# Products with the values for eight heads in one visit, five load buffers and nine probability tiles

## The chip, the cores and the metric

The kernel runs on one core of a Trainium2 chip. The metric is the device time of one execution in microseconds (us), as the median of several runs. A core has five engines that run side by side, each with its own instruction stream: TensorE (PE; its weight loads are shown apart as PEld), VectorE (DVE), ScalarE (ACT), GpSimd (POOL) and SyncE (SP). They wait for one another by semaphores. Transfers between the large memory and the on-chip memory are issued by an engine and carried out by DMA engines. TensorE writes to PSUM, which the kernel uses as eight banks of 2 KB per partition; all else lies in the on-chip memory of 128 partitions.

## What is computed

The reference is a trunk of two layers over 256 tokens of 1024 numbers. Each layer takes a normalised input, projects it to all that three branches need, runs the branches, merges them by gates and adds the result. Cut to what matters here:

```python
for layer in range(2):
    h = rms_norm(x, norm_w[layer])
    proj = einsum('bsd,de->bse', h, w_in[layer])
    (a_xbc, a_z, a_dt, b_q, b_k, b_v, b_z,
     c_q, c_k, c_v, c_f, c_z, gates) = split(proj)
    y_a = mamba2_branch(...)                 # a chunked scan
    y_b = sliding_window_branch(...)         # 16 heads, window 128, sinks
    y_c = forgetting_attention_branch(...)   # 16 heads, causal, decay bias
    branch = einsum('bsiw,iwd->bsid', stack(y_a, y_b, y_c), w_proj[layer])
    x = x + einsum('bsd,de->bse', sum(g * branch), w_out[layer])
return rms_norm(x, final_norm_w)

# in both attention branches
probs = softmax(scores)
out = einsum(probs, v)
return out * silu(z)
```

Heads are 64 wide, so each attention branch has 16 heads of 256 queries. With blocks of 128 tokens a head has three blocks of probabilities: the first query block against the first key block, and the second against both.

## The kernel before

**Dense projections.** Nearly all of TensorE's time goes to the projections. Activations and weights are each split into a rounded high part and a rest, and each product is made of three: high by high, low by high, high by low (`dense`, L275, and `dense2`). A 1024-row weight matrix is taken in column pieces, and each piece in parts of 512 KB or less, 274 parts in all. A part goes through three steps: SyncE issues its load into a `raw` buffer (`load_part`, L321 to L332, the issue on L330); ScalarE rounds it into a `hi` buffer (L261); VectorE subtracts to make the `lo` buffer (L262). After that the raw buffer is free.

`feed` keeps four split parts ahead of TensorE (`AHEAD`), and after each split it asks `load_to` for the load of the part that is `N_RAW` further on. All loads are on SyncE's queue in the order of the parts, so load j waits for the lo of part j - `N_RAW`, and everything after it on that queue waits too. In the start (L1226, L1230) parts are split in halves.

**Side work.** Attention, the scan and the norms are written as generators. They are advanced between dense pieces, from `pump`, by a planner with a clock of its own in estimated microseconds: a generator yields either a delay, or the name of a token, or a condition, and is advanced when it is due and what it waits for holds. The order of TensorE's instructions that comes out of this is kept by the program. VectorE, ScalarE and GpSimd follow the written order only in the start; afterwards a scheduler sets theirs. In what follows, a stretch of side work on TensorE between two dense matmuls is called a visit.

**PSUM.** Dense results rotate over three banks (`pmm`), side work over five (`pmx`).

**Attention.** `attn_quad` (L534) handles four heads and is used 16 times: four times per layer by `swa_quad` (L611) for the sliding window and four times by `fox_quad` (L862) for the other. In order it

- takes the token `pp` (one for two buffers of scores), makes the scores in four PSUM banks with 64-row tiles in one visit;
- does the softmax: VectorE adds the bias and takes the extreme (L561), ScalarE the exponential (L567), VectorE scales (L579);
- transposes twelve 128x128 blocks in two visits of six, and ScalarE copies them to three tiles of 2 KB per partition (L596). These are tag `L2`, which the scan, the gates and others also use;
- gives `pp` back, then waits for `gated`, which says that the gate values for these heads are there;
- makes the products with the values in one bank `py`: 8 matmul instructions, each with 64 columns of weights, so that two heads go to the lower and upper half of the partitions;
- multiplies by the gate on VectorE (L609).

In the traces a product visit is recorded as 16 matmuls "mx<-L,L" with the tile shape 128*64 and 256 columns as the first record's shape.

**The scan.** `ssd_group` (L706) does four heads, eight groups in all over the two layers. It may begin when no sliding-window attention of its layer is waiting, and holds one token `ssd`. Its last visit has 24 records, also of 128*64, and takes a new bank four times. Where the text speaks of the third branch's attention, it is `fox_quad`'s.

**The end of a layer.** `out_end` adds the residual (L1003), squares (L217) and, after the last piece, normalises the rows for the next layer; its transposes and splits then feed the next layer's first dense matmuls.

Buffers are counted by tag in `BUFS` (L59).

Of the kernel before, what the change touches and what calls it, by code (L numbers as in the profile page):

```python
# [14 lines left out]
ALU = mybir.AluOpType  # L15

P = 128
S = 256
# [8 lines left out]
D_GN1, D_GN2, D_CUM, D_H, D_M = 4.0, 6.0, 12.0, (4.8, 6.4), 5.0  # L27
BUDGET = 1.35
T_PP, T_SSD, T_BIAS = 1, 1, 1
N_RAW, N_SPLIT = 6, 6  # L30
AHEAD = 4
WARM = 10
FILL = 10
# [11 lines left out]
def hybrid_trunk(  # L45
# [10 lines left out]
    ps = ctx.enter_context(tc.tile_pool(name="ps", bufs=1, space=bass.MemoryType.PSUM))  # L56
    dr = ctx.enter_context(tc.tile_pool(name="dr", bufs=1, space=bass.MemoryType.DRAM))

    BUFS = dict(raw=N_RAW, hi=N_SPLIT, lo=N_SPLIT, L8=8, L4=2, L2=7, L1=14, pp=2, qt=4,  # L59
                bias=2, st=2, sm=6)  # L60
    count = [0]

    def T(tag, shape, dtype=F32, bufs=None):
        count[0] += 1
        return sb.tile(shape, dtype, tag=tag, name=f"{tag}_{count[0]}",
                       bufs=bufs if bufs is not None else BUFS.get(tag, 1))

    def PS(tag, bufs):
        count[0] += 1
        return ps.tile([P, 512], F32, tag=tag, name=f"{tag}_{count[0]}", bufs=bufs)  # L70
# [4 lines left out]
    def pmx():  # L75
        return PS("mx", 5)
# [3 lines left out]
    tt = nc.vector.tensor_tensor  # L80
# [10 lines left out]
    def mm(o, a, b, **kw):  # L91
        n = b.free_size()
        if a.dtype == F32R:
            clock["t"] += max(0.094, n / 2350.0)
        else:
            clock["t"] += max(0.2, n / 587.0) * (0.5 if a.free_size() == 64 else 1.0)
        nc.tensor.matmul(o, a, b, **kw)  # L97

    def transpose(o, a, i):
        clock["t"] += 0.109  # L100
        nc.tensor.transpose(o, a, i)  # L101
# [91 lines left out]
    def bc(ap, axis, n):  # L193
        s = list(ap.shape)
        s.insert(axis, n)
        return ap.unsqueeze(axis).to_broadcast(s)
# [192 lines left out]
    for l in range(L):  # L389
        y = Layer()  # L390
# [140 lines left out]
            yield 0.0  # L531
        return f

    def attn_quad(qTs, kTs, biases, nsink, v, vcols, sz, gated, scored=lambda: None):  # L534


        yield "pp"
        pps = [T("pp", [P, 2, 3 * P]) for _ in range(2)]
        nm = T("nm", [P, 8], bufs=2)
        sums = T("sums", [P, 8], bufs=2)  # L540
        blocks = ((0, slice(0, P)), (1, slice(P, 3 * P)))

        scs = [pmx() for _ in range(4)]

        def score(p, i, b):
            return scs[2 * p + i][:, b * P:P + 2 * P * b]

        for p in range(2):
            for b in range(2):
                for i in range(2):  # L550
                    r = slice(64 * i, 64 * i + 64)
                    mm(score(p, i, b), qTs[p][r, b * P:(b + 1) * P], kTs[p][r, 0:(b + 1) * P],
                       start=True, stop=True)
        for p in range(2):
            pp = pps[p]
            ps_ = slice(4 * p, 4 * p + 4)
            ns = None if nsink is None else nsink[:, 2 * p:2 * p + 2]
            for i in range(2):
                for b, sl in blocks:
                    e = 4 * p + 2 * i + b  # L560
                    nc.vector.tensor_tensor_reduce(  # L561
                        out=pp[:, i, sl], in0=score(p, i, b), in1=biases(p, i, b), scale=-0.125,
                        scalar=1.0e30 if ns is None else ns[:, i:i + 1],
                        op0=ALU.add, op1=ALU.min, accum_out=nm[:, e:e + 1])
                for b, sl in blocks:
                    e = 4 * p + 2 * i + b
                    act(pp[:, i, sl], pp[:, i, sl], AF.Exp, scale=-1.0, bias=nm[:, e:e + 1],  # L567
                        accum_out=sums[:, e:e + 1])
            if nsink is not None:
                es = T("es", [P, 4], bufs=2)  # L570
                tt(es.rearrange("p (i b) -> p i b", i=2), nm[:, ps_].rearrange("p (i b) -> p i b", i=2),
                   bc(ns, 2, 2), op=ALU.subtract)
                act(es, es, AF.Exp)
                tt(sums[:, ps_], sums[:, ps_], es, op=ALU.add)
            rs = T("rsum", [P, 4], bufs=4)
            nc.vector.reciprocal(rs, sums[:, ps_])
            for i in range(2):
                for b, sl in blocks:
                    ts(pp[:, i, sl], pp[:, i, sl], rs[:, 2 * i + b:2 * i + b + 1], 0.5,  # L579
                       op0=ALU.mult, op1=ALU.mult)  # L580
        yield D_SOFT
        scored()

        order = [(0, 0), (0, 1), (1, 0), (1, 1), (0, 2), (1, 2),
                 (2, 0), (2, 1), (2, 2), (3, 0), (3, 1), (3, 2)]
        at = {hb: (n // 4, n % 4 * P) for n, hb in enumerate(order)}
        pTs = []
        for n, (h, b) in enumerate(order):
            if n == 6:
                yield D_SOFT2  # L590
            if n % 4 == 0:
                pt = pmx()
            transpose(pt[:, n % 4 * P:(n % 4 + 1) * P], pps[h // 2][:, h % 2, b * P:(b + 1) * P], ident)
            if n % 4 == 3:
                pT = T("L2", [P, 512])
                act(pT, pt, AF.Copy)  # L596
                pTs.append(pT)
        yield D_EVAC
        tokens["pp"] += 1
        yield gated  # L600
        sz = sz()
        py = pmx()
        for p in range(2):
            for b, o in ((0, 0), (1, P)):
                for i in range(2):
                    n, c = at[2 * p + i, 2 * b]
                    mm(py[64 * i:64 * i + 64, S * p + o:S * p + S], v[:, b, vcols(p, i)],
                       pTs[n][:, c:c + S - o], start=(b == 0), stop=(b == 1))
        tt(sz, py.rearrange("p (u s) -> p u s", u=2), sz, op=ALU.mult)  # L609

    def swa_quad(y, c, qT):  # L611
        yield lambda: (1, 0) in y.zdone or (y.l == 0 and y.rn is None)
        yield from attn_quad(
            [qT[:, j, :] for j in range(2)], [y.kT[:, c, :]] * 2,
            lambda p, i, b: wmask[:, P:2 * P] if b == 0 else wmask,
            y.nsink[:, 4 * c:4 * c + 4], y.bv, lambda p, i: slice(64 * c, 64 * c + 64),
            lambda: y.sz[1][:, 2 * c:2 * c + 2, :], lambda: (1, 2 * c + 1) in y.zdone)
# [244 lines left out]
    def fox_quad(y, j):  # L862
        yield "bias"
        bs = []
        for p in range(2):
            bias = T("bias", [P, 2, 3 * P])
            nc.scalar.dma_start(bias[:, :, P:3 * P],
                                y.cumd[2 * (j + p):2 * (j + p) + 2, 1, :].partition_broadcast(P))
            bs.append(bias)
        yield D_BDMA  # L870
        for bias in bs:
            for dst, src in ((slice(0, P), slice(P, 2 * P)), (slice(2 * P, 3 * P), slice(2 * P, 3 * P))):
                for i in range(2):
                    nc.gpsimd.affine_select(out=bias[:, i, dst], in_=bias[:, i, src],  # L874
                                            compare_op=ALU.is_ge, fill=NEG, base=0,
                                            pattern=[[-1, P]], channel_multiplier=1)
        yield lambda: j + 1 in y.cqdone and clock["t"] >= y.cqdone[j + 1] + D_BIAS
        kqs = [y.ckT[j], y.ckT[j + 1]]

        def scored():  # L880
            tokens["bias"] += 1

        yield from attn_quad([kq[:, 1, :] for kq in kqs], [kq[:, 0, :] for kq in kqs],
                             lambda p, i, b: bs[p][:, i, P * b:P + 2 * P * b], None, y.cv,
                             lambda p, i: slice(P * (j + p) + 64 * i, P * (j + p) + 64 * i + 64),
                             lambda: y.sz[2][:, j:j + 2, :], lambda: (2, j + 1) in y.zdone, scored)
# [169 lines left out]
    def sub(src, n=256):  # L1056
        subs.append((src, n))
        return len(subs) - 1
# [5 lines left out]
    for y in layers:  # L1064
# [2 lines left out]
        y.rn = None  # L1067
        y.gate, y.qT, y.ckT, y.sz, y.yh, y.yl, y.sq, y.h, y.ss, y.var, y.zdone, y.cqdone = {}, {}, {}, {}, {}, {}, [], {}, {}, {}, set(), {}
        y.u = y.cv = None

        def cols(c0, n=256):
            return sub([(0, w[:, c0:c0 + n])], n)
# [30 lines left out]
        if l == 0:  # L1103
            k, v = cols(C_BK), cols(C_BV)
# [47 lines left out]
        o = [sub([(0, w_out[l, :, c:c + n])], n) for c, n in ((0, 256), (256, 512), (768, 256))]  # L1152
# [36 lines left out]
    with tc.manual_schedule(engines={ENG.PE, ENG.DVE, ENG.Activation, ENG.Pool}):  # L1189
# [10 lines left out]
        p = pmx()  # L1200
# [90 lines left out]
        for k in (0, 2):  # L1291
# [4 lines left out]
        v = T("sm", [P, 8])  # L1296
        nc.vector.tensor_reduce(v[:, 0:2], ss.rearrange("p (t j) -> p t j", t=2), axis=mybir.AxisListType.X,
                                op=ALU.add)
# [51 lines left out]
```

## Time and profile before

| what | value |
|---|---|
| median of 3 runs | 840.01 us (839.77 to 840.1) |
| the profiled execution's own time | 839.45 us |
| span in that profile | 837.7 us |
| mean granted TensorE clock | 0.999 |
| split of raw parts to hi, L261 | 262 times, 264.1 us busy on ScalarE |
| rest to lo, L262 | 262 times, 312.7 us busy on VectorE |
| loads of 512 KB for the input projection | 179, median 4.6 us from issue to landing |
| moved by DMA | 157.99 MB, mean 189 GB/s |

The span is what the profile's rows cover; the execution's own time is 1.75 us longer. Rows of a timeline give the start in us from the span's start, the duration, the engine, line and operation, then out<-in with the names of the program, the shape of the tile and the columns, and the number of records put together in the row. In square brackets stands the idle time before it and what ended it. Rows of a window give the length of the stretch, then the busy time and the instructions (x) of the engines named, then granted clock, the DMA share and GB/s. Matmuls are pipelined and their ends are modelled, so durations of two matmuls overlap, and the differences between starts are what counts. Rows of waits give total us, number of times and longest.

### The profile page before, as it was taken

How to read it: one execution, taken by the hardware profiler on the slowest of the kernel's cores; microseconds unless marked ns; L12 is line 12 of the kernel's file. 1: busy time of each engine (PE TensorE's matmuls, PEld its weight loads, DVE VectorE, ACT ScalarE, POOL GpSimd, SP SyncE). 2: the span in 40 equal slices, each digit the busy share in tenths (PEclk: the TensorE clock that was granted, in tenths of full speed). 3: DMA queues.
4: the chain of work that ended last, by engine and by line, in shares of the span. 5: the costliest groups of instructions: out<-in, count | busy, mean ns of one | idle time of the engine just before them, and what ended most of it. 6: DMA issues, size and time to landing. Idle time of an engine off the chain costs nothing.

```text
span 837.7 us, 16280 instructions
## 1 busy us (share of the span) xinstructions
PE 828.7 (99%) x6067; PEld 767.2 (92%) x6067; DVE 650.2 (78%) x1426; ACT 510.9 (61%) x1022; POOL 102.3 (12%) x141
## 2 busy tenths in 40 slices
PE   8999999999999999999999999999999999999996
PEld 8999999989999998888999999999899999988896
DVE  6987898998766679665787688899968667785665
ACT  7477768665666657443654676876557567654442
POOL 1810000000221010220024000100003110121000
PEclk9999999999999999999999999999999999999999
DMA  9775467676565556665676544765756564476632
GB/s 307 220 216 169 119 185 229 204 214 203 153 198 176 153 165 203 207 221 186 211 247 213 152 121 147 226 216 187 247 175 183 155 189 151 153 238 214 214 101 76
DMA packets 123113, 157.99 MB, mean 189 GB/s; under 512 B 5746, under 2 KB 90090, under 8 KB 123034
## 3 DMA queue, kind: packets, MB, share of 16 engines
q1 hardware_dynamic: 108816, 140.53, 53.6%
q10 hardware_dynamic: 13962, 16.37, 6.2%
q8 instruction: 48, 0.79, 0.4%
q14 instruction: 31, 0.25, 0.1%
q0 software_dynamic: 256, 0.05, 0.0%
HBM read 154.76 MB, written 2.16 MB: 187 GB/s over the span
## 4 chain that ended last, share of the span: by engine, by line
PE 98%; DMA 1%; DVE 0%; SPq 0%; POOLq 0%; issue 0%; ACT 0%
PE mm L97 84%; PE mx L97 9%; PE mx L101 4%; DMA L<-in_x_dram 1%; SPq L330 0%; SPq L164 0%; DVE L L1214 0%; POOLq L1346 0%; ACT L L1028 0%; DVE L L1222 0%; DVE L L1003 0%; DVE L L1007 0%; DVE sm L230 0%; DVE rs L232 0%; DVE sm L256 0%
## 5 line engine op out<-in xcount | busy, mean ns | idle before, releaser
L262 DVE TENSOR_TENSOR lo<-raw,hi 128x1024 fp32r<-128x1024 f32 (+3 forms) x262 | 312.7, 1208 | 85.8 <-ACT hi L261 75.4
L97 PE MATMUL mm<-hi,L 128*128 128x512 f32 (+4 forms) x1424 | 376.5, 352 | 0.2
L97 PE MATMUL mm<-L,hi 128*128 128x256 f32 x1792 | 318.0, 279 | 0.0
L261 ACT ACTIVATE hi<-raw 128x1024 fp32r<-128x1024 f32 (+3 forms) x262 | 264.1, 1022 | 84.7 <-PE mm L97 76.6
L97 PEld LDWEIGHTS mm<-L,hi 128*128 128x128 f32 x1792 | 277.9, 192 | 7.4 <-issue 3.9
L97 PEld LDWEIGHTS mm<-hi,L 128*128 128x128 f32 x1424 | 251.0, 190 | 26.3 <-issue 2.1
L97 PE MATMUL mm<-lo,L 128*128 128x512 f32 (+4 forms) x712 | 247.1, 348 | 0.0
L97 PE MATMUL mm<-L,lo 128*128 128x256 f32 x896 | 246.7, 275 | 0.0
L97 PEld LDWEIGHTS mm<-L,lo 128*128 128x128 f32 x896 | 172.1, 192 | 0.2
L97 PEld LDWEIGHTS mm<-lo,L 128*128 128x128 f32 x712 | 134.6, 190 | 12.3
L874 POOL TENSOR_SCALAR_AFFINE_SELECT bias<-bias 128x128 f32<-128x128 f32 x64 | 34.1, 569 | 409.5 <-DMA bias<-cumd 291.1
L567 ACT ACTIVATE pp<-pp,nm 128x128 f32<-128x128 f32 (+1 forms) x128 | 56.6, 444 | 13.2 <-DVE nm L561 11.2
L696 DVE SCALAR_TENSOR_TENSOR L<-L,vec,L 128x255 f32<-128x255 f32 (+2 forms) x96 | 46.1, 481 | 2.1 <-ACT L L693 1.1
L699 ACT ACTIVATE L<-L 128x256 f32<-128x256 f32 x32 | 13.3, 417 | 41.1 <-DVE L L696 41.1
L898 ACT ACTIVATE L<-L 128x512 f32<-128x512 f32 x24 | 15.2, 631 | 36.5 <-DVE L L897 36.3
L97 PE MATMUL mx<-L,L 128*64 128x128 f32 (+1 forms) x384 | 34.5, 314 | 0.0
L579 DVE TENSOR_SCALAR pp<-pp,rsum 128x128 f32<-128x128 f32 (+1 forms) x128 | 32.3, 317 | 0.3
L780 ACT ACTIVATE L<-mm 128x256 f32<-128x256 f32 x48 | 18.1, 378 | 20.5 <-PE mm L97 20.5
L97 PEld LDWEIGHTS mx<-L,L 128*64 128x64 f32 x384 | 22.9, 136 | 8.3 <-issue 1.4
L596 ACT ACTIVATE L<-mx 128x512 f32<-128x512 f32 x48 | 26.8, 596 | 1.2 <-PE mx L101 1.0
L101 PE MATMUL mx<-ident,pp 128*128 128x128 f32 x192 | 26.3, 273 | 0.0
L897 DVE TENSOR_TENSOR L<-mm,L 128x512 f32<-128x512 f32 x24 | 16.5, 687 | 12.3 <-PE mm L97 12.3
(187 smaller groups left out, 726.6 us busy)
## 6 DMA issues: line engine op xcount, KB each, us to landing
raw<-in_w_in_dram SPq DMA_DIRECT2D x179, 512.0 KB, 4.6
raw<-in_w_proj_dram SPq DMA_DIRECT2D x48, 512.0 KB, 4.5
raw<-in_w_out_dram SPq DMA_DIRECT2D x16, 512.0 KB, 4.8
raw<-in_w_in_dram SPq DMA_DIRECT2D x16, 344.0 KB, 3.2
L<-cumd ACTq DMA_DIRECT2D x8, 512.0 KB, 5.0
bias<-cumd ACTq DMA_DIRECT2D x16, 256.0 KB, 3.6
L<-in_gate_bias_dram ACTq DMA_DIRECT2D x12, 256.0 KB, 5.2
raw<-in_w_in_dram SPq DMA_DIRECT2D x8, 352.0 KB, 3.3
```

The lines of the kernel that those rows point to most:

```text
L97: nc.tensor.matmul(o, a, b, **kw)
L101: nc.tensor.transpose(o, a, i)
L261: keep(act)(hi, src, AF.Copy)
L262: keep(tt)(lo, src, hi.bitcast(F32), op=ALU.subtract)
L567: act(pp[:, i, sl], pp[:, i, sl], AF.Exp, scale=-1.0, bias=nm[:, e:e + 1], accum_out=sums[:, e:e + 1])
L579: ts(pp[:, i, sl], pp[:, i, sl], rs[:, 2 * i + b:2 * i + b + 1], 0.5, op0=ALU.mult, op1=ALU.mult)
L596: act(pT, pt, AF.Copy)
L696: stt(a[:, s:S], x_[:, 0:S - s], y.vec[:, 16 * j + u:16 * j + u + 1], a[:, s:S], op0=ALU.mult, op1=ALU.add)
L780: act(halves(th), p, AF.Tanh, scale=0.5)
L874: nc.gpsimd.affine_select(out=bias[:, i, dst], in_=bias[:, i, src], compare_op=ALU.is_ge, fill=NEG, base=0, pattern=[[-1, P]], channel_mul ...
L897: tt(halves(g), p, halves(y.gb), op=ALU.add)
L898: act(g, g, AF.Tanh, scale=0.5)
```

## The change

The first quad of a pair no longer makes its products when its gate is there. It stores its gate condition, a function that makes the products, and its gate tile in a list `y.pair`, and ends. The second quad adds its own, takes both from the list, waits until both gates are there, makes the products of the first and of the second one after the other into two banks, and then does the two multiplies. Pairs are formed by the order in which quads come to this point, in each layer; there are two pairs per branch and layer.

Tag `L2` gets nine buffers instead of seven, that is 4 KB more per partition, and `raw` five instead of six, 4 KB less. Transposes, copies and the return of the token `pp` stay where they were in the generator.

```diff
-N_RAW, N_SPLIT = 6, 6
+N_RAW, N_SPLIT = 5, 6
...
-    BUFS = dict(raw=N_RAW, hi=N_SPLIT, lo=N_SPLIT, L8=8, L4=2, L2=7, L1=14, pp=2, qt=4,
+    BUFS = dict(raw=N_RAW, hi=N_SPLIT, lo=N_SPLIT, L8=8, L4=2, L2=9, L1=14, pp=2, qt=4,
...
-    def attn_quad(qTs, kTs, biases, nsink, v, vcols, sz, gated, scored=lambda: None):
+    def attn_quad(pair, qTs, kTs, biases, nsink, v, vcols, sz, gated, scored=lambda: None):
...
         yield D_EVAC
         tokens["pp"] += 1
-        yield gated
-        sz = sz()
-        py = pmx()
-        for p in range(2):
-            for b, o in ((0, 0), (1, P)):
-                for i in range(2):
-                    n, c = at[2 * p + i, 2 * b]
-                    mm(py[64 * i:64 * i + 64, S * p + o:S * p + S], v[:, b, vcols(p, i)],
-                       pTs[n][:, c:c + S - o], start=(b == 0), stop=(b == 1))
-        tt(sz, py.rearrange("p (u s) -> p u s", u=2), sz, op=ALU.mult)
+
+        def products_with_values():
+            py = pmx()
+            for p in range(2):
+                for b, o in ((0, 0), (1, P)):
+                    for i in range(2):
+                        n, c = at[2 * p + i, 2 * b]
+                        mm(py[64 * i:64 * i + 64, S * p + o:S * p + S], v[:, b, vcols(p, i)],
+                           pTs[n][:, c:c + S - o], start=(b == 0), stop=(b == 1))
+            return py
+
+
+        pair.append((gated, products_with_values, sz))
+        if len(pair) == 2:
+            quads = pair[:]
+            pair.clear()
+            yield lambda: all(g() for g, _, _ in quads)
+            for py, (_, _, own) in zip([f() for _, f, _ in quads], quads):
+                o = own()
+                tt(o, py.rearrange("p (u s) -> p u s", u=2), o, op=ALU.mult)
...
+        y.pair = []
```

`swa_quad` and `fox_quad` hand `y.pair` on to `attn_quad`.

More of the change, by code (lines that the diff above doesn't have):

```diff
@@ L613, in swa_quad @@
         yield from attn_quad(
-            [qT[:, j, :] for j in range(2)], [y.kT[:, c, :]] * 2,
+            y.pair, [qT[:, j, :] for j in range(2)], [y.kT[:, c, :]] * 2,
             lambda p, i, b: wmask[:, P:2 * P] if b == 0 else wmask,
@@ L881, in scored @@
             tokens["bias"] += 1
-        yield from attn_quad([kq[:, 1, :] for kq in kqs], [kq[:, 0, :] for kq in kqs],
+        yield from attn_quad(y.pair, [kq[:, 1, :] for kq in kqs], [kq[:, 0, :] for kq in kqs],
                              lambda p, i, b: bs[p][:, i, P * b:P + 2 * P * b], None, y.cv,
```

## The prediction

> **What bounds the kernel now.** I read the page's totals first, then the chain that ended last, and then TensorE's busy time by stage.
>
> ```profile
> PE 828.7 (99%) x6067; PEld 767.2 (92%) x6067; DVE 650.2 (78%) x1426; ACT 510.9 (61%) x1022; POOL 102.3 (12%) x141
> PE 98%; DMA 1%; DVE 0%; SPq 0%; POOLq 0%; issue 0%; ACT 0%
> core 0: us, PE busy (x), PEclk, DMA share, GB/s
> 0.00:15.00 15.00, 12.56 (x79) 1.00 0.90 303
> 15.00:831.00 816.00, 816.00 (x5991) 1.00 0.60 187
> 831.00:837.70 6.70, 0.12 (x2) 0.84 0.21 78
> ```
>
> TensorE is busy for 816.00 of the 816.00 us between 15 and 831, at granted clock 1.00. The chain that ends last is 98% PE. So a microsecond of TensorE time saved between 15 and 831 is a microsecond off the end, as long as everything that feeds it still comes in time; and what any other engine saves is worth nothing. Both ends (15.0 and 6.7 us) are left as they are by the change, apart from the loads at the start.
>
> **What the change removes.** TensorE runs the dense projections and is interrupted for short visits of attention and scan work. One visit with four heads' products, and the whole of one scan visit:
>
> ```profile
> 82.46 0.28 PE L97 MATMUL mm<-L,hi 128*128 128x256 f32 x1
> 82.67 1.52 PE L97 MATMUL mx<-L,L 128*64 128x256 f32 x16
> 84.12 0.38 PE L97 MATMUL mm<-L,hi 128*128 128x256 f32 x1
> 84.33 0.28 PE L97 MATMUL mm<-L,lo 128*128 128x256 f32 x1
> 84.44 0.39 PE L97 MATMUL mm<-L,hi 128*128 128x256 f32 x2
> ...
> 161.40 0.28 PE L97 MATMUL mm<-L,hi 128*128 128x256 f32 x1
> 161.61 0.88 PE L97 MATMUL mx<-L,L 128*64 128x128 f32 x12
> 162.31 0.39 PE L97 MATMUL mx<-L,st 128*64 128x128 f32 x4
> 162.53 0.39 PE L97 MATMUL mx<-L,L 128*64 128x128 f32 x4
> 162.75 0.39 PE L97 MATMUL mx<-L,st 128*64 128x128 f32 x4
> 163.07 0.38 PE L97 MATMUL mm<-L,hi 128*128 128x256 f32 x1
> 163.28 0.27 PE L97 MATMUL mm<-L,lo 128*128 128x256 f32 x1
> 163.39 0.28 PE L97 MATMUL mm<-L,hi 128*128 128x256 f32 x1
> ```
>
> Starts are exact while ends are modelled, so I take differences of starts. Dense 256-column matmuls follow each other at 0.11 us (84.33 to 84.44; a little finer, 0.112). From 82.46 to 84.44 three dense steps pass, so the visit costs TensorE 1.98 - 3 x 0.112 = 1.645 us more than no visit. The scan visit likewise costs 1.99 - 3 x 0.112 = 1.655.
>
> How much of this is fixed? In the scan visit four records take 0.22 us (162.31, 162.53, 162.75), so a pair of 64-column tiles with 128 columns takes 0.109 us. Its 24 records are 12 pairs, 12 x 0.109 = 1.31 us, which leaves 1.655 - 1.31 = 0.345 us for getting in and out. It can be seen at the edges: 82.46 to 82.67 and 84.12 to 84.33 are 0.21 us each, where a dense step is 0.112, so 0.10 is lost going in and 0.10 on the first dense matmul after; the other 0.15 is the first pair and the last. The product visit's content checks this: its pairs are four of 128 and four of 256 columns. With 0.216 us for 256 columns (the same per column), 4 x 0.109 + 4 x 0.216 = 1.30, and 1.30 + 0.345 = 1.645, which is what was measured.
>
> The changed program has eight runs of sixteen product instructions, each cut into two by hardware records as now, where there were sixteen runs of eight. The products are the same. Eight fixed costs go: 8 x 0.345 = **2.76 us**.
>
> One more edge moves. Where a scan visit is followed at once by a score visit, the two cost more than apart:
>
> ```profile
> 216.39 0.28 PE L97 MATMUL mm<-L,hi 128*128 128x256 f32 x1
> 216.59 1.58 PE L97 MATMUL mx<-qt 64*128 64x128 f32 x16
> 218.32 0.28 PE L97 MATMUL mm<-L,lo 128*128 128x256 f32 x1
> ...
> 234.23 0.28 PE L97 MATMUL mm<-L,hi 128*128 128x256 f32 x1
> 235.89 1.89 PE L97 MATMUL mx<-qt 64*128 64x128 f32 x16
> 237.93 0.28 PE L97 MATMUL mm<-L,lo 128*128 128x256 f32 x1
> ```
>
> Alone the score visit takes 1.93 us to the second dense matmul, less two dense steps 1.71; the scan visit alone 1.655; together 3.36. Joined they take 3.70 - 0.224 = 3.48, so the joint costs 0.12. In the changed order one such neighbourhood, in the first layer, is gone: **-0.12 us**. I find no new one.
>
> **What the change adds.** (a) *Waits in the doubled visit.* It takes two PSUM banks of the five that side work shares, and the second one must have been read by its last user, mostly a score read on VectorE (L561). Each quad's last two copies (L596) must be done too. The tightest places:
>
> ```profile
> 100.55 0.48 DVE L561 CUSTOM_DVE_ANT_0 pp<-mx,wmask,nsink 128x256 f32<-128x256 f32 x1
> 102.38 1.52 PE L97 MATMUL mx<-L,L 128*64 128x256 f32 x16
> 542.13 1.07 ACT L596 ACTIVATE L<-mx 128x512 f32<-128x512 f32 x2
> 545.66 1.52 PE L97 MATMUL mx<-L,L 128*64 128x256 f32 x16
> ```
>
> The score bank read from 100.55 is free at 101.03; a second bank would be wanted half a visit after the start at 102.38, about 103.7: 2.6 us to spare. The copies end at 543.20, 2.46 us ahead of the products. These are covers, not proofs, because the two quads of a pair now share one gate; I take **0**. Uncovered, a late bank costs what is left of VectorE's score reads, 1 to 2 us a visit. The first quad's products are delayed to the second's, and then only its three tiles of copies are held longer, for which there are two buffers more.
>
> (b) *Two multiplies in a row* (L609) instead of one after each visit: the same number, nothing of TensorE's waits on them before the branch's projection. **0**.
>
> (c) *Five load buffers, not six.* SyncE issues load j once the lo part of j-5, not j-6, has been taken, and all later loads queue behind that wait (it waits 181 times now, 435.8 us together):
>
> ```profile
> SPq L330 <- DVE lo L262: 435.8, 181, 12.0
> DMA to landing us min/median/max: 3.1/4.4/9.5
> 409.54 0.37 SPq L330 DMA_DIRECT2D raw<-in_w_in_dram  x1
> 417.35 1.50 SPq L330 DMA_DIRECT2D raw<-in_w_in_dram  x2
> 420.20 2.00 ACT L261 ACTIVATE hi<-raw 128x1024 fp32r<-128x1024 f32 x2
> 423.02 0.42 ACT L217 ACTIVATE L<-L 128x256 f32<-128x256 f32 x1 [0.82 <-DVE L L1003]
> 20.67 1.06 ACT L261 ACTIVATE hi<-raw 128x1024 fp32r<-128x1024 f32 x1 [0.34 <-DMA raw<-in_w_in_dram]
> 22.08 1.06 ACT L261 ACTIVATE hi<-raw 128x1024 fp32r<-128x1024 f32 x1 [0.36 <-DMA raw<-in_w_in_dram]
> ```
>
> Setting every load back to the release one part earlier leaves few places without room. The worst is the end of layer 1. The load issued at 409.54 is the one split second in the row at 420.20 (from about 421.15), and with five buffers it would take the turn of the next, 417.35. Then it has 3.8 us, and ScalarE has 0.82 us of idle time before the square at 423.02, on which the next layer's norm hangs. So it stalls TensorE by (landing time - 4.62): below nothing at 3.1 and at the median 4.4, and 4.9 us at the longest, 9.5. The next load, issued just then, is in the quieter part of the stretch; I take the median: **0**, upper end 4.9. At the start the engines move 303 GB/s with a DMA share of 0.90, so the loads arrive in a file whatever their issue, and ScalarE already waits 0.34 and 0.36 us for two of them without a TensorE wait after 15 us; **0**, upper end 1.0.
>
> The Trainium skill, "DMA: Bandwidth & Descriptors", section "Rules for kernel authors", advises issuing a DMA early and waiting for it late, which speaks against holding one load fewer. Its section "Anatomy of one DMA" fits 2.0 us plus bytes over 436 GB/s, for 512 KB an estimate of 3.2 us; by that the term at the layer's end would be nothing as well. The trace has 3.1 only as its least, so the rows decide.
>
> **Sum.** -2.76 - 0.12 + 0 = -2.88 us. The profiled execution took 839.45 us (span 837.7 and 1.75 around it), the median of the runs shown is 840.01, 0.56 more. 839.45 - 2.88 = 836.57 for a profiled execution, **837.1 us** for the median.
>
> **The rivals.**
>
> *1. The fixed cost comes back between the two quads.* The second quad starts a new PSUM bank and waits on other semaphores. If half of 0.345 recurs, 8 x 0.17 = 1.4 is kept and the time is 838.5; if all, 839.9; about **839.2**. Against it: by the code the scan visit changes its bank three times, and its rows at 162.31, 162.53 and 162.75 are 0.22 apart throughout. The Trainium skill, "TensorEngine Tiling (Array Packing)", section "Key Properties", says that changing the tiling mode drains the engine and changing only the tile does not. Both quads use one mode, and the scan rows agree.
>
> *2. VectorE falls behind in the first branches.* The scan may begin only when the second branch's attention is through, which now comes later, so more of the scan meets the third branch's softmax.
>
> ```profile
> core 0: us, PE busy (x) PEld busy (x) DVE busy (x) ACT busy (x) POOL busy (x), PEclk, DMA share, GB/s
> 100.00:250.00 150.00, 150.00 (x1183) 138.53 (x1180) 130.01 (x323) 98.46 (x216) 14.51 (x24) 1.00 0.64 195
> L696 DVE SCALAR_TENSOR_TENSOR L<-L,vec,L 128x255 f32<-128x255 f32 (+2 forms) x96 | 46.1, 481 | 2.1 <-ACT L L693 1.1
> ```
>
> VectorE is busy 130.01 of 150 us here, 87%, so 20 us are free and a burst that is too late by the length of two convolutions (three such operations each, 6 x 0.48 = 2.9) would use up the gain: **840.0**. For it speaks this share; against it, that TensorE loses nothing there now and the later quads get more time for their softmax.
>
> *3. Slower: the weights come late.* If the load at the end of layer 1 takes the longest landing time seen and the start loses its 1.0, the stalls are 5.9 us: 840.01 - 2.88 + 5.9 = **843.0**. It decides from a landing time of 7.5 us there (4.62 + 2.88), and shows as slower from 9.2. For it: this stretch is the one with the norm on the path, and the longest landing times are real. Against it: the median is 4.4.
>
> That the change doesn't do what it says is excluded by the order of the changed program, which TensorE keeps.
>
> **How the numbers follow.** My forecast has a chance of 0.62, the first rival 0.12, the second 0.11, the third 0.15. A change of 0.2%, 1.7 us, is about what a measurement of this kernel can tell from none: faster means under 838.3, slower over 841.7. The forecast is faster (0.62), the first two are within (0.23), the third is slower (0.15). Alone the forecast would range from 836.4 to 838.0, a gain of 3.6 (if other edges move by 0.7) to 2.0; for 8 in 10 the range takes in both rivals within the bound and the lower part of the third: 836.4 to 841.4.
>
> **What would show it.** Right: eight product visits of about 2.95 us (1.645 + 1.30) from the dense matmul before to normal cadence after; starts inside a visit without a gap over 0.22 us at its middle; busy 100% from 15 on and the last dense matmul 2.9 us earlier. Wrong by rival 1: a gap in the middle of each visit. By rival 2: gaps in front of transposes or scan visits between 100 and 250. By rival 3: idle TensorE at the layer's end with ScalarE's split waiting for a raw load there. A time over 838.3 makes the forecast wrong.

## The result, and the profile after

| | before | changed |
|---|---|---|
| median of 22 runs | 839.56 us (839.04 to 840.34) | 841.22 us (839.71 to 844.34) |
| ratio, 95% interval | 1 | 1.0022 (1.0016 to 1.0029) |
| profiled execution, its own time | 839.45 us | 839.71 us |
| end of TensorE's last matmul in it | 831.1 us | 831.4 us |

The changed kernel is 1.7 us slower, not 2.9 us faster, and its times spread over 4.6 us, where those of before lie within 1.3. The profile happens to be that of its fastest execution, so what it shows lost is the least.

First the page of the changed kernel, its totals and the chain that ended last, and then TensorE's busy time by stage in the same kernel (length, busy time and instructions, clock, DMA share, GB/s):

```profile
PE 827.7 (99%) x6067; PEld 766.6 (91%) x6067; DVE 651.6 (78%) x1426; ACT 510.3 (61%) x1022; POOL 100.5 (12%) x141
PE 89%; DVE 6%; ACT 2%; issue 1%; DMA 1%; POOL 1%; POOLq 0%; ACTq 0%; DVEq 0%
```

```profile
100.00:250.00 150.00, 150.00 (x1194) 1.00 0.64 196
400.00:430.00 30.00, 29.79 (x189) 1.00 0.80 265
430.00:640.00 210.00, 208.56 (x1608) 1.00 0.59 183
640.00:812.00 172.00, 171.71 (x1196) 1.00 0.60 186
```

TensorE's share of the chain went from 98% to 89%; VectorE, which had 0%, has 6%. TensorE is no longer busy throughout from 15 us on. The visits themselves are as forecast (TensorE's timeline of the changed kernel, one of the eight doubled visits):

```profile
263.51 0.28 PE L97 MATMUL mm<-L,hi 128*128 128x256 f32 x1
263.72 2.82 PE L97 MATMUL mx<-L,L 128*64 128x256 f32 x32
266.47 0.38 PE L97 MATMUL mm<-L,hi 128*128 128x256 f32 x1
266.68 0.28 PE L97 MATMUL mm<-L,lo 128*128 128x256 f32 x1
...
505.46 0.28 PE L97 MATMUL mm<-L,hi 128*128 128x256 f32 x1
505.67 3.16 PE L97 MATMUL mx<-L,L 128*64 128x256 f32 x32
508.75 0.38 PE L97 MATMUL mm<-L,hi 128*128 128x256 f32 x1
```

From 263.51 to 266.68 are 3.17 us, less two dense steps of 0.112 the visit costs 2.95, exactly 1.645 + 1.30. In seven of the eight there is no gap; in the one at 505.67 the second bank came 0.34 us late (3.29 us to the next dense matmul, not 2.96); what ended the wait was a score read on VectorE (L562, L561 before). In the first layer the saving can be read off whole. The dense matmul that starts at 71.28 us before, ahead of all pairs, starts at 70.71 in this profile; the one at 420.49, ahead of the layer's end, starts at 418.48. Between the two lie 1.44 us less, and four pairs with the joint of the prediction should give 1.50. So the saving came in, and was given back later on.

### Where it went

The largest stall is at 568 us. Both kernels do the same work on VectorE and ScalarE there: a convolution tile's three multiply-adds (L696 before, L707 after), its tanh behind them on ScalarE (L699, L710), and behind that on ScalarE the copy that empties the next dense PSUM bank (L693, L704). Between the first and the second multiply-add VectorE's order has `ds`, the first operation that reads a scan group's decay load `L<-cumd` (512 KB, issued by ScalarE). Before, in the timelines of VectorE, ScalarE and TensorE:

```profile
565.10 0.48 DVE L696 SCALAR_TENSOR_TENSOR L<-L,vec,L 128x255 f32<-128x255 f32 x1
565.49 0.16 DVE L724 TENSOR_TENSOR ds<-L,acum 128x4 f32<-128x4 f32 x1
565.61 0.48 DVE L696 SCALAR_TENSOR_TENSOR L<-L,vec,L 128x254 f32<-128x254 f32 x1
```

```profile
560.62 0.37 ACTq L711 DMA_DIRECT2D L<-cumd  x1
...
567.72 0.42 ACT L699 ACTIVATE L<-L 128x256 f32<-128x256 f32 x1 [1.42 <-DVE L L696]
568.04 0.36 ACT L692 ACTIVATE L<-mm 128x256 f32<-128x256 f32 x1
568.30 0.56 ACT L693 ACTIVATE L<-mm,vec 128x256 f32<-128x256 f32 x1
```

```profile
569.61 0.28 PE L97 MATMUL mm<-L,hi 128*128 128x256 f32 x1
569.72 0.60 PE L97 MATMUL mm<-hi,L 128*128 128x512 f32 x2
```

The bank is empty at 568.86 and TensorE wants it at 569.72: 0.86 us of room, and no gap anywhere. The same three timelines of the changed kernel:

```profile
563.58 0.47 DVE L707 SCALAR_TENSOR_TENSOR L<-L,vec,L 128x255 f32<-128x255 f32 x1
566.06 0.16 DVE L735 TENSOR_TENSOR ds<-L,acum 128x4 f32<-128x4 f32 x1 [2.01 <-DMA L<-cumd]
566.14 0.48 DVE L707 SCALAR_TENSOR_TENSOR L<-L,vec,L 128x254 f32<-128x254 f32 x1
```

```profile
560.27 0.42 ACTq L722 DMA_DIRECT2D L<-cumd  x1
...
568.24 0.42 ACT L710 ACTIVATE L<-L 128x256 f32<-128x256 f32 x1 [1.78 <-DVE L L707]
568.56 0.37 ACT L703 ACTIVATE L<-mm 128x256 f32<-128x256 f32 x1
568.82 0.56 ACT L704 ACTIVATE L<-mm,vec 128x256 f32<-128x256 f32 x1
```

```profile
567.84 0.28 PE L97 MATMUL mm<-L,hi 128*128 128x256 f32 x1
569.43 0.70 PE L97 MATMUL mm<-hi,L 128*128 128x512 f32 x2 [1.32 <-ACT L L704]
```

TensorE is there 1.77 us earlier (567.84 for 569.61; 0.57 of it was there already at 71 us), and VectorE's first multiply-add 1.52 earlier. But the decay load was issued only 0.35 us earlier and landed later, so VectorE stands still for 2.01 us in front of `ds`, with the second multiply-add behind it, ScalarE's tanh behind that, and the copy that TensorE needs behind the tanh. The copy ends at 569.38, half a microsecond later than before. TensorE loses 1.48 us and, with the slower first matmul after, 1.6.

Counted from the issue of the load it becomes a sum. From `ds` to the end of the copy it takes 3.4 us before and 3.3 here. TensorE wants the bank 9.1 us after the issue before (560.62 to 569.72) and 7.7 here (560.27 to 567.95); `ds` starts 4.9 us after the issue before, without a hold, and 5.8 here. So TensorE comes 1.4 us sooner and `ds` 0.9 later, 2.3 in all, of which the room of 0.86 takes up its part and the stall is the rest.

### The profile page after: what moved, and what is told of

It is laid out like the page before. It is cut to its first block, busy times and chain, and to the rows that moved or that the text cites. A ratio compares the mean times of both kernels' runs of the same rounds, so it can differ in the third digit from the quotient of the medians.

```text
span 838.0 us, 16279 instructions
## 1 busy us (share of the span) xinstructions
PE 827.7 (99%) x6067; PEld 766.6 (91%) x6067; DVE 651.6 (78%) x1426; ACT 510.3 (61%) x1022; POOL 100.5 (12%) x141
## 4 chain that ended last, share of the span: by engine, by line
PE 89%; DVE 6%; ACT 2%; issue 1%; DMA 1%; POOL 1%; POOLq 0%; ACTq 0%; DVEq 0%
PE mm L97 76%; PE mx L97 8%; PE mx L101 5%; DVE lo L262 2%; ACT hi L261 1%; DMA L<-cumd 1%; DVE L L707 1%; DVE L L262 0%; ACT pp L568 0%; POOL sm L817 0%; DVE L L1045 0%; DVE L L745 0%; DVE L L1014 0%; DVE uq L658 0%; POOL sm L228 0%
## 5 line engine op out<-in xcount | busy, mean ns | idle before, releaser
L707 DVE SCALAR_TENSOR_TENSOR L<-L,vec,L 128x255 f32<-128x255 f32 (+2 forms) x96 | 46.0, 479 | 1.5 <-ACT L L704 0.6
L710 ACT ACTIVATE L<-L 128x256 f32<-128x256 f32 x32 | 13.4, 418 | 39.8 <-DVE L L707 35.5
L908 DVE TENSOR_TENSOR L<-mm,L 128x512 f32<-128x512 f32 x24 | 16.5, 686 | 12.8 <-PE mm L97 11.4
```

Of the source, the lines that this page charges most:

```text
L707: stt(a[:, s:S], x_[:, 0:S - s], y.vec[:, 16 * j + u:16 * j + u + 1], a[:, s:S], op0=ALU.mult, op1=ALU.add)
L908: tt(halves(g), p, halves(y.gb), op=ALU.add)
```

## The experiments

Lines of `attn_quad` and after are numbered 11 higher in kernels with pairs (L707 is L696 of before, L735 is L724).

### Which part of the change costs

Five load buffers alone:

```diff
-N_RAW, N_SPLIT = 6, 6
+N_RAW, N_SPLIT = 5, 6
```

> The kernel before with five load buffers alone (no pairs, seven L2 tiles); all engines keep the order of the kernel before. If late weights made the change slow, they cost the 1.7 us it lost and the 2.9 us it should have gained, so this one is 3 to 4.6 us slower than before (ratio 1.004 to 1.0055). If the cause is in the pairing, through VectorE being held by the scan's decay load, this one is level with before (0.999 to 1.001).

Measured 839.79 us against 839.58, ratio 1.0001 (0.9992 to 1.0010). The sixth buffer is worth nothing here; late weights are not the cause.

The pairs alone, the changed kernel with six load buffers and seven L2 tiles (`N_RAW` 6, `L2=7`), and with five and seven:

> Pairs alone: six load buffers and seven L2 tiles as before. Late weights as cause: the whole 2.9 us come in, ratio 0.9965. VectorE held by the decay load: the TensorE stall of about 1.5 us near 568 us is still there, the time differs from run to run by several us, and the ratio is 1.000 to 1.002.

> The changed kernel with seven L2 tiles in place of nine. If the two more tiles are needed to hold the pairs' probabilities, this one is slower than the changed kernel by waits of the copies (over 842 us); if not, it is level with it (841.2, or ratio 1.001 to 1.003). Against the run with six buffers it gives the price of the buffer with pairs.

Measured 843.04 us, ratio 1.0037 (1.0025 to 1.0050), and 842.88 us, 1.0036 (1.0024 to 1.0049). Both are slower than the size given for the second theory (1.000 to 1.002), but the buffer again makes no difference, and the pairs alone hold the whole loss. The run with seven tiles and five buffers lies on the side (over 842) that its expectation gave to copies that wait for tiles; in its profile, though, TensorE has the same two stalls as the other, of 1.61 and 2.18 us, both behind L704. The first one's TensorE waits have two stalls of the kind above:

```profile
PE mm L97 <- ACT L L704: 3.6, 2, 2.1
```

One is near 568 us, the other near 137, where the first layer's scan begins. With nine L2 tiles the interval (1.0016 to 1.0029) overlaps these two, so that the extra tiles help is likely but not settled.

Pairs in one branch only:

```diff
-        if len(pair) == 2:
+        if len(pair) == (2 if nsink is None else 1):
```

> Pairs in the third branch (forgetting attention) only, with six load buffers and seven L2 tiles as before; four fixed visit costs go, 4 x 0.345 = 1.4 us. If the loss comes from the sliding-window pairs, which pull the dense work forward just where the scan's decay loads hold VectorE (near 137 and 568 us), this one shows no stall there and gains: 838.2 to 839.2 us, ratio 0.9985 to 0.9997 (some 0.5 us may be lost near 742). If pairing as such costs, it shares the loss of the run with all pairs: ratio 1.0015 to 1.0025.

> Pairs in the sliding-window branch only, six load buffers, seven L2 tiles. If the loss comes from these pairs, both stalls, near 137 and 568 us, are there in full and the time is that of the run with all pairs or above: 843 to 844.5 us, ratio 1.0035 to 1.006. If pairing as such costs: ratio 1.0015 to 1.0025.

(The sliding-window version has `is not None`; both have `N_RAW` 6 and `L2=7`.) Measured 839.67 us, ratio 0.9999 (0.9990 to 1.0009), and 843.29 us, 1.0043 (1.0030 to 1.0056). The sliding-window pairs, next to which the scan starts, carry the loss: their TensorE waits are

```profile
PE mm L97 <- ACT L L704: 3.0, 2, 2.2
```

The other branch's pairs should have gained 1.4 us and gained nothing that can be told. In TensorE's timeline of that run two gaps stand, one in each layer, that before doesn't have:

```profile
331.00 0.48 PE L97 MATMUL mm<-hi,L 128*128 128x512 f32 x1 [0.21 <-DVE L L262]
...
742.06 0.48 PE L97 MATMUL mm<-hi,L 128*128 128x512 f32 x1 [0.20 <-DVE L L262]
```

Each costs 0.37 us and 0.1 on the next matmul, 0.9 of the 1.4 us. They wait for VectorE's low parts of activations, at the projection that follows the scan's norms; how that chain got late was not taken apart.

### Does the same kernel vary because of the load?

The changed kernel once more, unedited:

> The changed kernel once more, for a second profile, since the first was of its fastest execution (839.71 us, where the median is 841.2). If the spread comes from how soon the scan's decay loads land, a slower execution shows the stall near 568 us again and a second one near 137 us, each longer where the load that VectorE waits for took longer; if it comes from the clock or the end of the kernel, the stalls are as in the first profile.

This execution took 842.01 us, 2.3 more than the first. `ds` of the layer's first group in VectorE's timeline, first in the first profile of the changed kernel and then in this one, with the one near 568 us in this one:

```profile
128.16 0.15 DVE L735 TENSOR_TENSOR ds<-L,acum 128x4 f32<-128x4 f32 x1
```

```profile
130.22 0.16 DVE L735 TENSOR_TENSOR ds<-L,acum 128x4 f32<-128x4 f32 x1 [1.60 <-DMA L<-cumd]
...
568.37 0.17 DVE L735 TENSOR_TENSOR ds<-L,acum 128x4 f32<-128x4 f32 x1 [2.26 <-DMA L<-cumd]
```

and TensorE's timeline in it:

```profile
138.72 0.70 PE L97 MATMUL mm<-hi,L 128*128 128x512 f32 x2 [1.31 <-ACT L L704]
...
571.75 0.70 PE L97 MATMUL mm<-hi,L 128*128 128x512 f32 x2 [1.99 <-ACT L L704]
```

Where the first profile had no hold, VectorE is now held for 1.60 us, and a second stall of TensorE is there. (In the first profile the copy there ended at 136.60, 0.27 us before TensorE wanted the bank.) The granted clock was 0.998 in both executions, so the difference between these two isn't the clock's. At this place the kernel before had room: its copy (L693) started at 137.96 and TensorE wanted the bank at 140.09. In this run the copy starts at 138.11, as late as before, but TensorE wants the bank 2.8 us earlier, at 137.25. The kernel before was itself held 2.23 us for this load and did not notice:

```profile
127.88 0.16 DVE L724 TENSOR_TENSOR ds<-L,acum 128x4 f32<-128x4 f32 x1 [2.23 <-DMA L<-cumd]
```

That is the case in one place: the pairs move dense work ahead of VectorE's and ScalarE's by up to three microseconds, the room was 1.6, and a hold that used to vanish in it comes out. Near 568 us TensorE is only 0.13 us earlier than before in this execution, since the first stall has eaten the gain, and it stalls all the same: it wants the bank 7.3 us after the issue of the load, and `ds` starts some 6 us after it. What counts there is the distance to the load, not to the start of the kernel.

The books of this execution, from the shifts of dense matmuls: the visits give 2.9; the two stalls take 1.6 and 2.3, the late second bank 0.3, the place near 742 (here 744) 0.5 and the layer's end 0.3, together some 4.9 and a net 2.0. It took 2.6 more than the profiled execution of before; the remaining 0.6 lies in small steps, mostly around the norms after 716 us, that I did not resolve.

### Taking the hold away

Three L4 tiles, so that a group's decay load need not wait until the group two before it has been read; L2 goes back to seven, since memory is full:

```diff
-    BUFS = dict(..., L4=2, L2=9, ...)
+    BUFS = dict(..., L4=3, L2=7, ...)
```

> Pairs, five load buffers, seven L2 tiles, and three L4 tiles in place of two, so that the decay load of a scan group no longer waits until the exponentials of the group two before it have been read. TensorE keeps the changed kernel's order. VectorE held by the decay load: the stall near 568 us goes, and the ratio falls to 0.998 or less. Late weights: the ratio stays at 1.002 or so.

Measured 840.19 us, ratio 1.0006 (0.9998 to 1.0015), just below the changed kernel's interval (from 1.0016), and well below the run with two L4 tiles and the same seven L2 (1.0024 to 1.0049). ScalarE's timeline has the third group's load at

```profile
527.76 0.37 ACTq L722 DMA_DIRECT2D L<-cumd  x1
```

35.5 us before its place (563.3) in that other run, and VectorE's has its reader without a hold:

```profile
567.27 0.16 DVE L735 TENSOR_TENSOR ds<-L,acum 128x4 f32<-128x4 f32 x1
```

The stall there falls to 0.25 us. So the hold in front of the decay load is what makes the stall near 568 us, and without it this kernel is 2.7 us faster than with two L4 tiles. It isn't the gain that was expected of this run: the first group's load follows the store it reads, a free tile doesn't help it, and the stall near 137 us is still there (TensorE's timeline):

```profile
139.19 0.70 PE L97 MATMUL mm<-hi,L 128*128 128x512 f32 x2 [1.15 <-ACT L L704]
```

To bring that load forward, the cumulative sums it comes from were planned earlier, on top of the edit above:

```diff
-D_GN1, D_GN2, D_CUM, D_H, D_M = 4.0, 6.0, 12.0, (4.8, 6.4), 5.0
+D_GN1, D_GN2, D_CUM, D_H, D_M = 4.0, 6.0, 10.5, (4.8, 6.4), 5.0
```

> The kernel with pairs, five load buffers, seven L2 and three L4 tiles, and the planner's delay before the cumulative sums 10.5 in place of 12.0, which puts their products some 1.5 us of dense work earlier in TensorE's order, and with them the store and the first decay load of the layer. If that load's landing sets the stall near 137 us (1.4 us with three L4 tiles), the stall shrinks by up to 1.5 us: 838.4 to 839.5 us, ratio 0.9985 to 0.9998. If not: 840.2 as with three L4 tiles alone, ratio 1.0005.

Measured 843.75 us, ratio 1.0043 (1.0030 to 1.0056): worse. In its profile the stall near 137 us did shrink, from 1.15 to 0.68 us of idle time. But the products now wait 0.4 us at 117 for what they read, VectorE takes its work in another order, and a stall of another kind appears at 160 us, where TensorE waits for VectorE's addition for the gates (L908), which also empties a dense bank, as TensorE's waits show:

```profile
PE mm L97 <- DVE L L908: 2.0, 1, 2.0
```

The other way, to plan the first reader of the load later, in the changed kernel with nine L2 tiles:

```diff
+        yield 4.0
         ds = T("ds", [P, 4], bufs=2)
```

> The changed kernel with a planned delay of 4 us in the scan group between its decay load with the transposes and the first VectorE operation that reads the load, so that less is queued behind a load that hasn't landed. The scan visits come 4 us later in TensorE's order. If VectorE held by the load is the cause, the stall near 568 us goes or shrinks to under 0.5 us, waits of VectorE for the decay load fall from 4.6 us, and the time is 838 to 840 us, ratio 0.998 to 1.0005. If VectorE is simply short of time there, whatever it waits for, the stall stays and the ratio is 1.002 or above.

Measured 841.32 us, ratio 1.0018 (1.0009 to 1.0028). The stall near 568 us shrank to 0.7, a little above the size expected, but one of 1.3 us stands near 137, VectorE's waits for the load rose to 6.3 us, and small new gaps stand in four other places, where the scan's visits came to lie. It settles nothing.

A smaller load, one head's decay for all four heads of a group (the scan's values are then those of one head):

```diff
-        nc.scalar.dma_start(bcg, y.cumd[4 * g:4 * g + 4, 0, :].partition_broadcast(P))
+        nc.scalar.dma_start(bcg[:, 0:1, :], y.cumd[4 * g:4 * g + 1, 0, :].partition_broadcast(P))
...
-                stt(dec[:, h, :], bcg[:, h, tk], y.acum[:, c, 4 * g + h:4 * g + h + 1], negtri,
+                stt(dec[:, h, :], bcg[:, 0, tk], y.acum[:, c, 4 * g:4 * g + 1], negtri,
```

> The changed kernel, but each scan group loads the decay of one head (128 KB) in place of four (512 KB) and uses it for all four, so the scan's values are those of one head. TensorE's order is the same; VectorE's differs in places. If late decay loads cost what the pairs save, the waits of VectorE for them fall below 1 us in all, both stalls fall away and the gain of the visits shows: 837 to 838.7 us, ratio 0.997 to 0.999. If VectorE is merely short of time: 1.001 or above.

> The same edit of the decay load in the kernel before (values of one head for all four). There no stall of TensorE stands behind these loads, so whatever the theory nothing is gained: ratio 0.999 to 1.001. A gain of over 1 us would mean that the loads cost something in other ways as well.

(`ds` and the exponential `cx` read one head likewise.) Measured 840.77 us, 1.0013 (1.0004 to 1.0022), and 840.27 us, 1.0008 (0.9998 to 1.0017). A miss: the waits did not fall below 1 us. VectorE's waits have

```profile
DVE ds L735 <- DMA L<-cumd: 4.9, 3, 4.3
```

and the longest stands at the second layer's first group, whose load was issued at 521.14 and read at 525.56, so the smaller load took 4.4 us there. The edit also changed VectorE's order: the second group's `ds` now stands directly behind the first's. The stall near 568 us did fall below 0.5, that near 137 to 1.1. As the order changed too, and the kernel before came out 0.6 us slower with the edit (the interval includes no change), the two runs bound nothing.

### Is VectorE only short of time?

Two of the convolution's three multiply-adds left out, 64 operations or 30 us of VectorE's time (the convolution then has two taps of four):

```diff
-            for j in (2, 1, 0):
+            for j in (0,):
```

> The changed kernel with two of the three multiply-adds of the convolution on VectorE left out (64 operations of 0.48 us in all, 15 us a layer); the convolution has two taps in place of four. TensorE's order stays. If VectorE is short of time in the stretches where the pairs pull the dense work forward, both stalls (near 137 and 568 us) shrink below 0.5 us and the gain of the visits shows: 837 to 838.7 us, ratio 0.997 to 0.999. If single loads that land late decide, the stalls stay at 1 to 2 us: ratio 1.000 to 1.002.

> The same two multiply-adds left out in the kernel before. TensorE has no such stalls there, so nothing is gained: 839.3 to 840 us, ratio 0.9995 to 1.0005, whatever the cause. A gain of over 1 us would mean that VectorE holds TensorE in places that the profile doesn't show as stalls.

> The kernel with pairs, five load buffers, seven L2 and three L4 tiles, with the two multiply-adds left out. Both cures together: if time on VectorE and the late decay load together make the loss, this is the fastest: 836.8 to 838.2 us, ratio 0.9968 to 0.9985. If the order in which VectorE takes its work matters more than its amount, it stays over 839.

Measured 839.56 us, ratio 0.9997 (0.9989 to 1.0006); 839.42, 0.9999 (0.9990 to 1.0008); and 838.95, 0.9994 (0.9985 to 1.0003). In the kernel before the work is worth nothing, as expected. In the changed kernel it is worth the loss but not the gain. Both stalls are gone, though VectorE is still held by the load near 568 us, for 2.63 us: with less work behind it the hold no longer reaches TensorE. The profile has a new hold and a new stall, in VectorE's timeline and then TensorE's:

```profile
149.92 0.16 DVE L735 TENSOR_TENSOR ds<-L,acum 128x4 f32<-128x4 f32 x1 [5.16 <-DMA L<-cumd]
```

```profile
159.67 0.35 PE L97 MATMUL mm<-L,hi 128*128 128x256 f32 x1 [1.70 <-DVE L L908]
```

The second group's decay load is issued at 142.78 here, in the first profile of the changed kernel at 131.06, and VectorE is held by it for 5.16 us. That this hold makes the stall 10 us later is not shown: VectorE is idle once more in between, for 1.64 us, waiting for ScalarE. Neither theory of that run stands alone: the stall near 568 us needs the hold and the work behind it, and taking away either one all but removes it. The version with both cures has the lowest median of all kernels here, and no single stall above 0.5 us in its profile, but its interval includes no change, and it leaves out part of the computation. It is also 2.3 us short of the 2.9 that the visits save. By the shifts of dense matmuls its profiled execution gains 1.2 us, 0.5 in the first layer and 0.6 in the second; stalls of 0.3 to 0.5 us, near 160, 170 and 740, take part of the rest. So the two large stalls aren't all that the pairs cost. No complete version beat the kernel before.

### How far can the load buffers go?

Four of them, with nine L2 and three L4 tiles, which together fill the memory:

```diff
-N_RAW, N_SPLIT = 5, 6
+N_RAW, N_SPLIT = 4, 6
```

> All pairs, nine L2 tiles, three L4 tiles, and four load buffers, one fewer still. TensorE's order is the changed kernel's. If the two stalls make the loss and one goes with each pair of spare tiles, both shrink and the time falls below before: 837.5 to 839 us, ratio 0.9975 to 0.9995. If fewer load buffers cost something after all, this one with four is the worst of the paired kernels: over 1.003.

Measured 843.54 us, ratio 1.0046 (1.0032 to 1.0059). The stall near 568 us is 0.25, as with three L4 tiles before, so the cure works again, but now the weights are late. ScalarE's waits, ScalarE's timeline and two rows of TensorE's:

```profile
ACT hi L261 <- DMA raw<-in_w_in_dram: 13.3, 13, 1.9
```

```profile
424.95 1.06 ACT L261 ACTIVATE hi<-raw 128x1024 fp32r<-128x1024 f32 x1 [1.93 <-DMA raw<-in_w_in_dram]
```

```profile
429.44 1.32 PE L101 MATMUL mx<-ident,L 128*128 128x128 f32 x8 [1.34 <-DVE L L1045]
...
567.17 0.35 PE L97 MATMUL mm<-L,hi 128*128 128x256 f32 x1 [1.56 <-DVE L L908]
```

The split at 424.95 is the one at the end of the first layer that the prediction named for five buffers: the square of the norm (L217) stands directly behind it on ScalarE, and the next layer's transposes (429.44) wait for that norm. One buffer fewer than five, and it is there. It is half of what this run loses against the one with five buffers and three L4 tiles: the layer's end takes 1.7 us more by the shifts of dense matmuls, and another 1.8 goes at 567.17, where TensorE waits for L908. Why L908 is late there was not taken apart; VectorE has no hold by a decay load before it.

## Why the prediction was wrong

The time, 841.22 us, lies at the upper end of the range given (836.4 to 841.4), but the forecast was 837.1 and faster. That the range holds it is luck: its upper part was put in for late weights, which didn't come. By its own steps:

- **The visits: right.** 2.95 us each, and no gap between the quads in seven of eight; the first rival fell. The first layer's 1.44 us fit the 1.50 that four pairs and the joint should give. Only in one visit did the second bank, which was taken at 0, cost 0.34 us.
- **Five load buffers at 0: right.** The run with them alone is level, so the third rival fell at five. Its mechanism and place were right for four, for half of that run's loss. The 3.2 us for a load that the prediction gives beside its sum doesn't describe these loads, which before landed 3.1 us after their issue at the least and 4.4 at the median; the sum didn't use it.
- **What feeds the dense work: the step that failed.** The prediction said that a microsecond saved on TensorE is a microsecond off the end "as long as everything that feeds it still comes in time", and then checked this for the visits and the loads alone. It did not check the copies that empty the dense banks (L693). Their room in the kernel before can be read off: 0.86 us at 569.72 and 1.57 us at 140.09 (140.09 less 137.96 and 0.56). At the first of these places TensorE comes 1.4 us sooner after the issue of the load that VectorE is held by, and the load's reader 0.9 later; at the second, in the second profile, TensorE comes 2.8 us earlier. The two stalls alone take from 1.6 us (the first profile) to 3.8 (the second), where the forecast had 0.
- **The second rival was nearest,** at 840.0 and a chance of 0.11: VectorE, in the stretch from 100 to 250. It argued from the share of 87%, and priced a burst. What the runs show in its place is order: VectorE stands idle at a load that hasn't landed, with work that TensorE needs queued behind. It was also placed in the first layer only, while the larger stall is in the second, at the same point of the layer; and the stalls stand in front of dense matmuls, and not of transposes or scan visits, where the prediction would have looked for this rival.
- **"TensorE loses nothing there now" was taken as evidence against it.** It showed that the room was enough, not how much there was. The hold of 2.23 us was in the kernel before already.

What stays open: why the gaps near 331 and 742 us come with the other branch's pairs, why L908 is late in three of the runs, where the rest of the saving goes when both large stalls are away, and whether nine L2 tiles are worth anything.

## What to carry to other kernels

On an engine that is busy all the time, a saving is worth no more than the room that its feeders have; so before booking it, look up for each place behind the saving when the buffer it needs is ready and when it is wanted, and compare the difference with the shift. Where a load stands in the way, count the shift from its issue, since the load need not move with the consumer. Idle time of a feeder in front of a load is a warning even if nobody waits for it yet: what stands behind it in that engine's order can be late for a consumer that comes earlier. A spread that grows from run to run, here from 1.3 to 4.6 us, can be a sign that such room is gone; that it is narrow shows nothing, for the kernel with four load buffers has stalls at four places and times within 0.5 us in its five runs.

## What the runs showed of the hardware that was not expected

The same load in the same program takes differently long. VectorE's first `ds` starts 4.3 us after the issue of its 512 KB load in the first profile of the changed kernel, without a hold; in the second profile it was held until 130.22, 5.8 us after the issue.

A stall can cost TensorE its clock as well. In the profile of the pairs alone (six load buffers, seven L2 tiles), TensorE stood still for 2.05 us up to 573.11, and a little later the granted clock fell to a half for 3.4 us, from 574.4 to 577.8. TensorE's busy time in two stretches of that profile (then the clock, the DMA share and GB/s):

```profile
574.00:578.00 4.00, 4.00 (x18) 0.57 0.64 181
578.00:582.00 4.00, 4.00 (x34) 1.00 0.76 220
```

Dense matmuls of 512 columns follow each other at 0.43 us there in place of 0.22, and the stretch costs 1.6 us on top of the stall. In the other profiles, with stalls of up to 2.23 us, it is not there, and what decides was not tested. One such stretch lowers the mean granted clock of an execution by 0.5 x 3.4 / 840 = 0.002. Seven of the changed kernel's 22 executions have a mean clock of 0.996, the other fifteen 0.997 to 0.999. The seven took 841.83 to 844.34 us, median 842.38; the fifteen 839.71 to 842.15, median 840.83. So the spread goes with the clock as well as with the loads. None of the seven was profiled, so that they have such a stretch is likely but not shown. Without them the changed kernel is still 1.3 us slower than before.
